# A prefix log-sum-exp kernel: the own-total addition moved from VectorE to TensorE, Ln put ahead of Exp, and the last step joined to the pipeline

## Chip, cores, metric

One core of one Trainium2 chip. The time is device microseconds of one execution; the reported figure is the median of several. Executions of one kernel agree within about 0.3%, so differences of 1 us need several rounds.

## The reference

```python
def reference(x):                      # x: (4, 4096, 4128) float32
    out[:, 0, :] = x[:, 0, :]
    for t in range(1, S):
        mx = np.maximum(out[:, t - 1, :], x[:, t, :])
        out[:, t, :] = mx + np.log(np.exp(out[:, t - 1, :] - mx) + np.exp(x[:, t, :] - mx))
```

It is a running log-sum-exp along the sequence. The kernel computes it as Exp, prefix sum, Ln. 270.5 MB go in and 270.5 MB come out.

## The kernel before

A step is 384 rows of one batch (four of the 44 steps have 256): partition p holds three consecutive rows, so a partition's own rows are summed on VectorE (DVE), and the sum over the partitions above comes from TensorE (PE) with a triangular matrix. Four column chunks of 1024 make a step; the last 32 columns ("tail") ride with one of them. Four step buffers; all transfers are issued from SyncE (SP).

```python
        def own(self):
            r = self.t.r
            full = tpool.tile([P, CH + tail], FP32R, name="tot")     # 2 buffers
            self.tot = full[:, :self.b - self.a]
            for j in range(1, r - 1):
                add(self.row(j), self.row(j - 1), self.row(j))
            add(self.tot, self.row(r - 2), self.row(r - 1))          # total of a partition
        # head():  PSUM above[c] (+)= excl.T @ tot   (and pick.T @ carry for the last chunk)

        def sums(self, a, b, p, cr):
            t = self.t
            n = t.r - 1
            if n:
                v = t.xt[:, :n, a:b]
                add(v, v, p.unsqueeze(1).to_broadcast(v.shape))      # all rows but the last
            add(t.xt[:, n, a:b], self.tot[:, a - self.a:b - self.a], p)   # last row: DVE
            if cr is not None and not t.final:
                nc.vector.tensor_copy(cr[96:, :], t.xt[96:, n, a:b])      # carry, from SBUF
        # complete():  PSUM above[c] += rest.T @ tot   (ready for the next step)
        ...
    for part in (steps[:-1], steps[-1:]):          # the last step is a drain of its own
        chunks = [Chunk(s, c) for s in part for c in order]
        N = len(chunks)
        for g in range(-2, N + 1):
            if 0 <= g + 2 < N:
                chunks[g + 2].act(ACT.Exp)         # may wait for a load
            if 0 <= g + 1 < N:
                chunks[g + 1].own()
                chunks[g + 1].head()
            if 0 <= g < N:
                chunks[g].add_above()
                ...
                chunks[g].complete()
            ...
            if 0 <= g - 1:
                result(chunks[g - 1])              # Ln; after a step's last chunk: store, next load
```

The softmax here doesn't subtract the row's maximum and nothing guards it: scores larger than these inputs give would overflow.

## Time and profile before

| | before |
|---|---|
| median of the first three runs | 1265.25 us (1265.19 to 1268.24) |
| span of the profiled run | 1262.5 us |
| busy DVE / ACT / PE | 81% / 73% / 38% |
| HBM traffic over the span | 429 GB/s |

A busy share is an average and says nothing of who waits for whom. Here I add only the landing of the last full step's load (the moment its data have arrived, and the first Exp on them starts) and the two last stores on SP's queue (columns: start us, duration us, queue and line, operation, tile):

```profile
1197.23 2.84 ACT L118 ACTIVATE xt<-xt 128x3168 f32<-128x3168 f32 x1 [7.74 <-DMA xt<-in_x_dram]
```

```profile
1231.79 0.33 SPq L106 DMA_DIRECT2D out_dram<-xt  x1
```

```profile
1250.60 0.33 SPq L106 DMA_DIRECT2D out_dram<-xt  x1
```

The span ends 11.9 us after the last of them.

### The profile page before, as it was taken

To read this page: it belongs to the slowest core of one execution; us is meant where nothing else is said; L and a number is where in the kernel's file an instruction comes from. 1 tells how busy PE (TensorE), PEld (TensorE's weight loads), DVE (VectorE), ACT (ScalarE), POOL (GpSimd) and SP (SyncE) were. 2 spreads that over 40 slices of the span, in tenths; PEclk is the share of its full clock that TensorE was granted. 3 is DMA by queue.
4 is the path that set the end of the run, shared out by engine and by line. 5 is a ranking of instruction groups with operands and counts; after the bars stand their busy time and mean duration, and the time that the engine had idled before them with its cause. 6 is when DMAs were issued, how large, how long until landed. Compare 5 with 4: busy or idle time off the path is not lost.

```text
span 1262.5 us, 3545 instructions
## 1 busy us (share of the span) xinstructions
PE 480.5 (38%) x876; PEld 220.3 (17%) x876; DVE 1024.4 (81%) x858; ACT 921.0 (73%) x353; POOL 1.5 (0%) x10
## 2 busy tenths in 40 slices
PE   2445433333334434443324434443432443444332
PEld 1212111111111112211111112111111211111111
DVE  4999878888888888888679888887867988887784
ACT  4986677777777776668669776666966977666784
POOL 0000000000000000000000000000000000000000
PEclk9865555565555555556556565656555656555656
DMA  9999999999999999999999999999999999999997
GB/s 410 410 444 431 426 433 438 432 430 435 436 427 430 443 432 429 435 437 432 433 435 429 429 441 432 428 437 435 424 425 431 434 433 432 430 436 433 433 409 340
DMA packets 12692, 541.29 MB, mean 429 GB/s; under 512 B 1408, under 2 KB 1408, under 8 KB 1408
## 3 DMA queue, kind: packets, MB, share of 16 engines
q1 hardware_dynamic: 12672, 541.07, 99.4%
q8 instruction: 7, 0.11, 0.0%
q14 instruction: 13, 0.11, 0.0%
HBM read 270.53 MB, written 270.53 MB: 429 GB/s over the span
## 4 chain that ended last, share of the span: by engine, by line
DMA 69%; ACT 19%; issue 7%; DVE 3%; SPq 0%; PE 0%; DVEq 0%; ACTq 0%
DMA xt<-in_x_dram 63%; ACT xt L118 19%; DMA out_dram<-xt 6%; DVE xt L86 3%; DVE tot L86 1%; SPq L106 0%; PE above L83 0%; DVE carry L155 0%; DVEq L239 0%; ACTq L118 0%; DVE carry_t L155 0%; DVEq L86 0%
## 5 line engine op out<-in xcount | busy, mean ns | idle before, releaser
L118 ACT ACTIVATE xt<-xt 128x3072 f32<-128x3072 f32 (+3 forms) x352 | 919.7, 2692 | 328.8 <-DMA xt<-in_x_dram 315.0
L83 PE MATMUL above<-tot,excl 128*128 128x512 f32 (+1 forms) x396 | 255.1, 714 | 476.9 <-DVE tot L86 472.6
L86 DVE TENSOR_TENSOR xt<-xt,above 128x2048 f32<-128x2048 f32 (+3 forms) x220 | 393.4, 1788 | 0.0
L86 DVE TENSOR_TENSOR xt<-xt 128x1024 f32<-128x1024 f32 (+1 forms) x160 | 197.0, 1231 | 179.9 <-ACT xt L118 177.5
L86 DVE TENSOR_TENSOR tot<-xt 128x1024 fp32r<-128x1024 f32 (+1 forms) x176 | 217.1, 1234 | 40.4 <-ACT xt L118 18.9
L86 DVE TENSOR_TENSOR xt<-tot,above 128x1024 f32<-128x1024 f32 (+1 forms) x220 | 221.5, 1007 | 0.0
L83 PEld LDWEIGHTS above<-tot,excl 128*128 128x128 f32 x396 | 104.4, 305 | 607.4 <-DVE tot L86 566.9
L83 PE MATMUL above<-tot,rest 128*128 128x512 f32 x240 | 129.2, 633 | 205.1 <-DVE xt L86 205.1
L83 PE MATMUL above<-carry,pick 128*128 128x512 f32 x160 | 139.5, 972 | 0.0
L83 PEld LDWEIGHTS above<-tot,rest 128*128 128x128 f32 x240 | 53.1, 276 | 295.9 <-DVE xt L86 294.1
L83 PE MATMUL above<-carry_t,pick 128*128 128x32 f32 x80 | 25.2, 409 | 83.2 <-DVE xt L86 83.2
L83 PEld LDWEIGHTS above<-carry,pick 128*128 128x128 f32 x160 | 51.5, 322 | 11.1
L83 PEld LDWEIGHTS above<-carry_t,pick 128*128 128x128 f32 x80 | 20.2, 311 | 110.3 <-DVE xt L86 108.3
L155 DVE COPY carry<-xt 32x1024 f32<-32x1024 f32 x40 | 27.6, 691 | 1.4
L155 DVE COPY carry_t<-xt 32x32 f32<-32x32 f32 x40 | 7.1, 178 | 1.4
L63 ACT ACT_TABLE_LOAD x1 | 1.3, 1283 | 0.8 <-PEq L228 0.8
L77 DVE MEMSET carry<- 128x1024 f32 x1 | 0.9, 912 | 1.1 <-PEq L228 1.1
L24 POOL TENSOR_SCALAR_AFFINE_SELECT rest<-rest 128x128 fp32r<-128x128 f32 x1 | 0.3, 293 | 0.0
L24 POOL TENSOR_SCALAR_AFFINE_SELECT pick<-pick 128x128 f32<-128x128 f32 x1 | 0.3, 292 | 0.1
L24 POOL TENSOR_SCALAR_AFFINE_SELECT excl<-excl 128x128 fp32r<-128x128 f32 x1 | 0.3, 292 | 0.0
L23 POOL MEMSET excl<- 128x128 f32 x1 | 0.2, 204 | 0.3 <-POOLq L228 0.3
L23 POOL MEMSET rest<- 128x128 f32 x1 | 0.2, 204 | 0.0
(6 smaller groups left out, 0.7 us busy)
## 6 DMA issues: line engine op xcount, KB each, us to landing
xt<-in_x_dram SPq DMA_DIRECT2D x40, 6192.0 KB, 41.9
out_dram<-xt SPq DMA_DIRECT2D x40, 6192.0 KB, 27.7
xt<-in_x_dram SPq DMA_DIRECT2D x4, 4128.0 KB, 37.0
out_dram<-xt SPq DMA_DIRECT2D x4, 4128.0 KB, 25.4
```

The source lines that it names most:

```text
L23: nc.gpsimd.memset(t.bitcast(FP32), 1.0 - fill)
L24: nc.gpsimd.affine_select(out=t, in_=t, pattern=[[step, P]], compare_op=op, fill=fill, base=base, channel_multiplier=-step if step else 1,)
L63: nc.scalar.preload_act_table_set("natural_log_exp_and_others")
L77: nc.vector.memset(carry, 0.0)
L83: nc.tensor.matmul(o, lhsT=w, rhs=rhs, start=start, stop=True, skip_group_check=True)
L86: nc.vector.tensor_tensor(out=o, in0=a, in1=b, op=mybir.AluOpType.add)
L118: nc.scalar.activation(v, v, func)
L155: nc.vector.tensor_copy(cr[96:, :], t.xt[96:, n, a:b])
```

## The change

The intent: DVE, the busiest compute engine, should no longer add a partition's own total to the sum above. PE adds it into PSUM with an identity matrix, and ScalarE (ACT) reads the last row of Ln straight from PSUM. The old `rest` matrix (totals at and below) becomes `below`, applied after Ln has read. Ln is put ahead of the Exp that may wait for a load, and the last step is no longer a drain of its own.

```diff
-        select(FP32R, 0.0, ge, 0, -1, "rest"),
+        select(FP32R, 0.0, ge, -1, -1, "below"),
+        select(FP32R, 1.0, ne, 0, 1, "ident"),
 ... (tail total in a small tile of its own, tail sums in a function of their own)
-            add(t.xt[:, n, a:b], self.tot[:, a - self.a:b - self.a], p)
-            if cr is not None and not t.final:
-                nc.vector.tensor_copy(cr[96:, :], t.xt[96:, n, a:b])
+        def add_own(self):
+            self.banks(ident)
+        def keep(self):
+            if self.c == lastc and not self.t.final:
+                nc.vector.tensor_copy(carry[96:, :], above[lastc][96:, :])
+        def ln(self):
+            t, n, a, b = self.t, self.t.r - 1, self.a, self.a + CH
+            v = t.xt[:, :n, a:b]
+            nc.scalar.activation(v, v, ACT.Ln)
+            nc.scalar.activation(t.xt[:, n, a:b], above[self.c], ACT.Ln)
 ...
-    for part in (steps[:-1], steps[-1:]):
-        ... Exp(g+2); own, head(g+1); add_above(g); complete(g); Ln(g-1)
+    chunks = [Chunk(s, c) for s in steps for c in order]
+    for g in range(-2, N + 1):
+        ... ln(g-1); complete(g-1); store; exp(g+2); own(g+1); keep(g-1);
+            add_above(g); add_own(g); total(g+1); head(g+1)
```

More of the change, by code (lines that the diff above doesn't have):

```diff
@@ L64 @@
     consts = ctx.enter_context(tc.tile_pool(name="consts", bufs=1))
-    excl, rest, pick = _constants(nc, consts)
+    excl, below, ident, pick = _constants(nc, consts)
     bufs = 4
@@ L69 @@
     tpool = ctx.enter_context(tc.tile_pool(name="tpool", bufs=2))
+    upool = ctx.enter_context(tc.tile_pool(name="upool", bufs=1))
     cpool = ctx.enter_context(tc.tile_pool(name="cpool", bufs=1))
@@ L114, in row, with exp @@
             return self.t.xt[:, j, self.a:self.b]
-        def act(self, func):
+        def exp(self):
             v = self.t.xt[:, :, self.a:self.b]
-            nc.scalar.activation(v, v, func)
+            nc.scalar.activation(v, v, ACT.Exp)
         def own(self):
-            r = self.t.r
-            full = tpool.tile([P, CH + tail], FP32R, name="tot")
-            self.tot = full[:, :self.b - self.a]
-            for j in range(1, r - 1):
+            for j in range(1, self.t.r - 1):
                 add(self.row(j), self.row(j - 1), self.row(j))
-            add(self.tot, self.row(r - 2), self.row(r - 1))
@@ L129, in banks, with total @@
-        def banks(self):
+        def total(self):
+            x, r, a = self.t.xt, self.t.r, self.a
+            self.tot = tpool.tile([P, CH], FP32R, name="tot")
+            add(self.tot, x[:, r - 2, a:a + CH], x[:, r - 1, a:a + CH])
+            if self.c == firstc:
+                self.t.tot_t = upool.tile([P, tail], FP32R, name="tot_t")
+                add(self.t.tot_t, x[:, r - 2, t0:], x[:, r - 1, t0:])
+        def banks(self, w, cr=None, start=False):
             for s in range(0, CH, MM):
-                yield above[self.c][:, s:s + MM], s, s + MM
+                o = above[self.c][:, s:s + MM]
+                if cr is not None:
+                    mm(o, pick, cr[:, s:s + MM], start=True)
+                mm(o, w, self.tot[:, s:s + MM], start=start)
@@ L133, in head @@
         def head(self):
             through = self.c == lastc and not self.t.first
-            for o, s, e in self.banks():
-                if through:
-                    mm(o, pick, carry[:, s:e], start=True)
-                mm(o, excl, self.tot[:, s:e], start=self.t.first)
-        def tail_head(self):
-            if not self.t.first:
-                mm(above_t, pick, carry_t, start=True)
-            mm(above_t, excl, self.tot[:, CH:], start=self.t.first)
-        def sums(self, a, b, p, cr):
-            t = self.t
-            n = t.r - 1
-            if n:
-                v = t.xt[:, :n, a:b]
-                add(v, v, p.unsqueeze(1).to_broadcast(v.shape))
-            add(t.xt[:, n, a:b], self.tot[:, a - self.a:b - self.a], p)
-            if cr is not None and not t.final:
-                nc.vector.tensor_copy(cr[96:, :], t.xt[96:, n, a:b])
@@ L157, in add_above @@
-        def add_above(self):
-            self.sums(self.a, self.a + CH, above[self.c], carry if self.c == lastc else None)
-            if self.c == firstc:
-                self.sums(t0, D, above_t, carry_t)
+            self.banks(excl, carry if through else None, start=self.t.first)
+        def add_above(self):
+            t, n = self.t, self.t.r - 1
+            v = t.xt[:, :n, self.a:self.a + CH]
+            add(v, v, above[self.c].unsqueeze(1).to_broadcast(v.shape))
+        def add_own(self):
+            self.banks(ident)
@@ L162, in complete @@
+        def keep(self):
[6 more added lines that the diff above has]
+            nc.scalar.activation(t.xt[:, n, a:b], above[self.c], ACT.Ln)
         def complete(self):
             if self.c != lastc and not self.t.final:
-                for o, s, e in self.banks():
-                    mm(o, rest, self.tot[:, s:e])
+                self.banks(below)
@@ L168, with tail_sums @@
+    def tail_sums(t):
+        n = t.r - 1
+        if not t.first:
+            mm(above_t, pick, carry_t, start=True)
+        mm(above_t, excl, t.tot_t, start=t.first)
+        v = t.xt[:, :n, t0:]
+        add(v, v, above_t.unsqueeze(1).to_broadcast(v.shape))
+        add(t.xt[:, n, t0:], t.tot_t, above_t)
+        if not t.final:
+            nc.vector.tensor_copy(carry_t[96:, :], t.xt[96:, n, t0:])
     steps = []
@@ L184 @@
     stored = 0
-    def result(k):
-        nonlocal stored
-        k.act(ACT.Ln)
-        if k.c == lastc:
-            k.t.store()
-            if bufs <= stored + ahead < len(steps):
-                steps[stored + ahead].load()
-            stored += 1
-    for part in (steps[:-1], steps[-1:]):
-        chunks = [Chunk(s, c) for s in part for c in order]
-        N = len(chunks)
-        for g in range(-2, N + 1):
-            if 0 <= g + 2 < N:
-                chunks[g + 2].act(ACT.Exp)
-            if 0 <= g + 1 < N:
-                chunks[g + 1].own()
-                chunks[g + 1].head()
-            if 0 <= g < N:
-                chunks[g].add_above()
-                if g + 1 < N and chunks[g + 1].c == firstc:
-                    chunks[g + 1].tail_head()
-                chunks[g].complete()
-            elif g == -1:
-                chunks[0].tail_head()
-            if 0 <= g - 1:
-                result(chunks[g - 1])
+    chunks = [Chunk(s, c) for s in steps for c in order]
+    N = len(chunks)
+    for g in range(-2, N + 1):
+        if 0 <= g - 1:
+            k = chunks[g - 1]
+            k.ln()
+            if k.c == order[1]:
+                v = k.t.xt[:, :, t0:]
+                nc.scalar.activation(v, v, ACT.Ln)
+            k.complete()
+            if k.c == lastc:
+                k.t.store()
+                if bufs <= stored + ahead < len(steps):
+                    steps[stored + ahead].load()
+                stored += 1
+        if g + 2 < N:
+            chunks[g + 2].exp()
+        if 0 <= g + 1 < N:
+            chunks[g + 1].own()
+        if 0 <= g - 1:
+            chunks[g - 1].keep()
+        if 0 <= g < N:
+            chunks[g].add_above()
+            chunks[g].add_own()
+            if chunks[g].c == order[1]:
+                tail_sums(chunks[g].t)
+        if 0 <= g + 1 < N:
+            chunks[g + 1].total()
+            chunks[g + 1].head()
 _INS = ['x']
```

## The prediction

> **What bounds the kernel now.** I read the page's DMA rows first, then the busy table, who waited for whom, and last the stretches of time at both ends.
>
> ```profile
> span 1262.5 us, 3545 instructions
> PE 480.5 (38%) x876; PEld 220.3 (17%) x876; DVE 1024.4 (81%) x858; ACT 921.0 (73%) x353; POOL 1.5 (0%) x10
> ...
> DMA  9999999999999999999999999999999999999997
> ...
> HBM read 270.53 MB, written 270.53 MB: 429 GB/s over the span
> ...
> L86 DVE TENSOR_TENSOR xt<-tot,above 128x1024 f32<-128x1024 f32 (+1 forms) x220 | 221.5, 1007 | 0.0
> ```
>
> DVE at 81% looks like the engine to relieve, and the last line is the work that the change takes from it. But the DMA row is at nine tenths in every slice but the last. The stretches say how near to its limit that is (columns: stretch, length, busy PE, PEld, DVE, ACT, POOL with counts, then PE clock, DMA share, GB/s):
>
> ```profile
> 97.00:1197.00 1100.00, 425.71 (x772) 194.43 (x772) 904.04 (x751) 803.29 (x304) 0.00 (x0) 0.56 1.00 433
> ...
> 1229.00:1231.00 2.00, 0.00 (x0) 0.00 (x0) 0.00 (x0) 2.00 (x1) 0.00 (x0) 0.50 0.34 149
> ...
> 1232.00:1246.00 14.00, 7.41 (x15) 3.71 (x15) 11.60 (x12) 10.89 (x6) 0.00 (x0) 0.58 1.04 449
> ...
> 1247.00:1250.00 3.00, 0.00 (x0) 0.00 (x0) 1.57 (x2) 2.65 (x2) 0.00 (x0) 1.00 0.04 17
> ```
>
> For 1100 us the queue runs at 433 GB/s and never pauses. It does pause at the end, twice: about 1228.7 to 1232.3 and 1246.6 to 1251.0 (read from half-microsecond stretches), because there the next store has not been issued. Who waits confirms it:
>
> ```profile
> ACT xt L118 <- DMA xt<-in_x_dram: 315.0, 41, 12.4
> ...
> DVE xt L86 <- ACT xt L118: 177.5, 35, 12.2
> ```
>
> ACT idles some 7.7 us in each step for a load, DVE behind it. A full step moves 2 x 6.34 MB (6192 KB in, the same out); at 433 GB/s this is 29.3 us, and loads do land 29.25 us apart (ACT starts on them at 1108.58 and 1137.83).
>
> How much queue is left when ACT is late? The load landing at 1197.2 (call it L) and the store queue near it:
>
> ```profile
> 1184.13 0.33 SPq L106 DMA_DIRECT2D out_dram<-xt  x1
> 1184.52 0.42 SPq L103 DMA_DIRECT2D xt<-in_x_dram  x1
> ```
>
> A load lands 42 us after its issue (page, transfers), of which only 14.6 are its own at 433 GB/s: the rest is queue. With the store issued 13 us before a landing and the following load right behind it, about 29 us of work is queued when a load lands; the next store comes 16.2 us later (1213.37 - 1197.2). So some 13 us of queue remain at the leanest moment of a step. Compute is not on the path in the middle; it is only at the end, where no load is left.
>
> **What the Trainium skill says.** "DMA: Bandwidth & Descriptors", section "Where 436 GB/s comes from", gives 435 GB/s as the ceiling of the 16 SBUF ports. The 433 GB/s measured here agrees: nothing on compute engines can raise it. "ScalarE: Activation LUTs", section "What ACT_TABLE_LOAD costs", gives 186 ns + 0.833 ns per element for an activation with immediates, and 93 ns overlap of neighbours. This trace: 1896 ns at 2048, 2748 at 3072 (formula 1892 and 2745), and eight in a row take 21.50 us where their own durations sum to 22.17, so 96 ns of overlap. Thus 1024 elements should take 1.04 us, 96 should take 0.27; whether a PSUM source costs the same no run shows. "TensorE: Matmul & The Clock Gate", section "What's actually happening", says that the array clock halves unless PE has lately been busy; here the mean granted clock is 0.584 and a pair of 512-column matmuls takes 1.22 us at half clock, 0.73 right after the carry matmuls.
>
> **The change part by part.**
> (1) Removed from DVE: 176 adds tot + above of 1214 ns = 213.6 us. Added: 44 small tail totals of 0.18 = 8 us; the 44 totals of 1258 shrink to 1225 (-1.5). DVE falls from 1024 to about 819 us, 24 to 19 us per step. All of it lies beside DMA: worth 0 in the middle.
> (2) PE gains 352 identity matmuls with 352 weight loads. At 633 to 756 ns (the rest and excl groups) that is +220 to +265 us, PE near 720 us, 57%. It is below the transfers' time, but in the chain: the second Ln of a chunk waits for it.
> (3) ACT: each Ln of 3072 (2.75) becomes 2048 from SBUF (1.90) and 1024 from PSUM (1.04); the tail becomes a separate 0.27. Per full step 13 activations: 2.84 + 3 x 2.75 + 4 x 2.94 + 0.27 = 23.1, less 12 overlaps of 0.095 = 22.0 us against 21.5 now; ACT some 950 us in all. Hidden under 29.3.
> (4) The sum below now waits for Ln of the same chunk (it overwrites what Ln reads), and the next total but one needs the buffer that it frees. A new ring: total 1.2, excl 1.2, add 2.3, identity 1.2, Ln 1.0 to 2.9, below 1.2. It spans two chunks, about 10 us, so 5 per chunk.
> (5) Ln goes ahead of Exp. A store now comes after the load's landing + Exp 2.84, Ln 2.9, Exp 2.7, Ln 2.9 = 11.3 us instead of 16.2. In the middle this only lengthens the queue from 13 to 18 us. The load behind it then waits for the previous store's landing, about L + 14.8, which is still in time.
> (6) The last step is no longer a drain of its own.
>
> Middle: I walked one step through the orders of the engines by hand with the durations above, from a landing at 0. Ln of the four chunks start at 14.0, 19.6, 26.3, 33.3 (the second and third held up by the tail's matmuls and adds and by the carry matmuls), the first again one step later at about +26. So 26 of 29.3 us: DMA-bound as before, with less room than the busy times suggest.
>
> Start: the first store waits now for Exp of the second load before its last Ln: 41.3. By the same walk it comes at about 37.8, and the dip to 264 GB/s at 56 to 58 may fill: -0.7 us at most.
>
> End, where time can change, counted from L = 1197.2. The queue then holds work until L + 31.5 (drained at 1228.7), in both kernels. The last load lands at L + 24.3 (37.0 us after 1184.5). Walk of the changed kernel: last full step's second chunk, Ln to 22.8; Exp of the last step 24.3 to 26.3; Ln of the third chunk to 29.2; carry and excl matmuls of the fourth to 31; add to 33.2; Ln 33.3 to 36.2. Store at L + 36.2; before, 1231.8 = L + 34.6. It fills the queue from 36.7 to 51.1 (14.4 as before). Then the last step, three and more rounds of total 1.2 + excl 1.2 + add 1.2 with handoffs, the tail's 1.7, the carry matmuls 3.3, ending with Ln in two parts at L + 55.6; before, 1250.6 = L + 53.4. Its store moves data from 56.0 to 65.6 (9.6 as before), and the end is 1.9 later: 67.5 against 65.3 now.
>
> Sum: 0 (middle) - 0.7 (start) + 2.2 (end) = +1.5 us: 1265.25 + 1.5 = 1266.75; I say 1266.5.
>
> **Rivals.**
> (a) The end becomes better: Exp of the last step can start at its load's landing, not 10 us later. If nothing else held, both gaps (3.6 and 4.4 us) would close: 1257. For it: order of Exp. Against: the chain runs over DVE and PE, in order, not over Exp. A faster PE clock under more matmuls would take about 1 us off.
> (b) The new ring with its PE handoffs exceeds 29.3 us a step (it has 26 by hand; each of four chunks would need 0.8 us more, for instance by an Ln from PSUM far above 1.04). Then the bound moves from DMA to the ring, and 1 us of excess costs 40 us: 1300. Against: all but the PSUM Ln are measured durations, and DVE and ACT each have over 7 us of idle.
> (c) Freed DVE time shows in full (1024 - 819, so 5 us a step): 1060. This needs more than 435 GB/s; excluded by the DMA row.
>
> **Range and chances.** Spread of before is 3 us; my walk may be off by 3 us either way at the end. Range 1260 to 1272. A 2% gain is 1240, below the 1250 that 541 MB at 433 GB/s take alone (541.07 / 0.433 = 1249.6): 1%. Slower by 2% needs (b): 2%. Within: 97%.
>
> **What would show it.** DMA share 1.00 and 433 GB/s from 97 to 1197 again; DVE near 819, PE near 720, ACT near 950; more ACT idle waiting for loads per step or about the same (some 7 us); stores 11 to 12 us after the landing; first store near 38; at the end two DMA pauses of about 5 us, not 3.6 and 4.4. I am wrong if the loads' spacing departs from 29.25 us, if ACT waits for PE in the middle rather than for loads, or if the two pauses close.

## The result, and the profile after

| | before | after |
|---|---|---|
| median | 1265.22 us (4 runs) | 1266.87 us (4 runs, 1266.13 to 1267.86) |
| ratio, 95% interval | 1 | 1.0009 (0.9991 to 1.0028): the same |
| span of the profiled run | 1262.5 | 1264.4 |
| DVE / ACT / PE busy us | 1024.4 / 921.0 / 480.5 | 853.3 / 940.5 / 653.6 |

Ratios here and below are the mean of one kernel's fast runs over the mean of the other's fast runs of the same rounds, so they are not quite the ratio of the medians quoted. The experiments ran in three groups, two on one chip and the third (carry copy, total twice, pieces without the additions on PE) on another; each group has its own runs of the kernel before.

The page of the changed kernel: busy engines, the DMA row, and the groups that carry the change.

```profile
PE 653.6 (52%) x1228; PEld 331.8 (26%) x1228; DVE 853.3 (67%) x726; ACT 940.5 (74%) x573; POOL 1.9 (0%) x12
...
DMA  9999999999999999999999999999999999999997
...
L85 PE MATMUL above<-tot,ident 128*128 128x512 f32 x352 | 204.8, 681 | 336.3 <-DVE xt L88 336.0
L163 ACT ACTIVATE xt<-xt 128x2048 f32<-128x2048 f32 (+1 forms) x176 | 321.0, 1824 | 69.6 <-DVE xt L88 69.3
...
L164 ACT ACTIVATE xt<-above 128x1024 f32<-128x1024 f32 x176 | 177.5, 1008 | 0.9 <-PE above L85 0.9
...
L158 DVE COPY carry<-above 32x1024 f32<-32x1024 f32 x40 | 49.2, 1230 | 53.8 <-ACT xt L164 53.8
```

DVE lost 171 us of work and the DMA row did not change by a digit. The stretches of the changed kernel (columns as in the prediction), to be held against those of before:

```profile
97.00:1195.00 1098.00, 576.06 (x1080) 292.69 (x1079) 756.29 (x639) 823.59 (x498) 0.00 (x0) 0.56 1.00 433
...
1229.00:1232.00 3.00, 1.32 (x4) 0.44 (x4) 1.28 (x3) 3.00 (x3) 0.00 (x0) 0.99 0.15 66
1232.00:1247.00 15.00, 8.58 (x17) 4.89 (x18) 8.33 (x9) 9.48 (x9) 0.00 (x0) 0.50 0.98 423
1247.00:1253.00 6.00, 2.87 (x6) 0.79 (x4) 1.22 (x1) 1.97 (x2) 0.00 (x0) 0.78 0.04 17
```

The same 433 GB/s and share 1.00 for 1098 us, then two pauses again (66 and 17 GB/s). The landing and the two last stores of the changed kernel:

```profile
1195.72 2.85 ACT L120 ACTIVATE xt<-xt 128x3168 f32<-128x3168 f32 x1 [6.89 <-DMA xt<-in_x_dram]
```

```profile
1231.74 0.33 SPq L108 DMA_DIRECT2D out_dram<-xt  x1
```

```profile
1252.48 0.33 SPq L108 DMA_DIRECT2D out_dram<-xt  x1
```

The last but one is issued at the same time as before (1231.79), the last one 1.9 us later than 1250.60. The spans differ by 1.9 us. That is where the whole difference of the two traces lies. (The load of the last full step happened to land 1.5 us earlier, at 1195.72 instead of 1197.23, so counted from the landing both stores are later: 36.0 and 56.8 us against 34.6 and 53.4.)

What sets the time between that landing and the last store is in the chain of work that ended last (window 1198 to 1252 us; "issue" is time without a wait that the profile shows), first before, then changed:

```profile
by line: DVE xt L86 47.9%; ACT xt L118 15.8%; DVE tot L86 13.8%; issue 13.8%; DVE carry L155 2.6%; PE above L83 2.3%; DVEq L239 2.1%; DVE carry_t L155 0.3%; DVEq L86 0.2%; ACTq L118 0.1%
by line: PE above L85 40.0%; DVE xt L88 27.3%; ACT xt L163 12.5%; DVE tot L88 6.7%; issue 6.7%; ACT xt L164 5.1%; DVE carry L158 4.6%; ACTq L254 1.7%; DVE carry_t L180 0.3%; ACTq L163 0.1%
```

Before, it is mostly DVE, and PE has 2% of it; in the changed kernel PE has 40%.

### The profile page after: what moved, and what is told of

The parts are those of the page before. It is cut to its first block, busy times and chain, and to the rows that moved or that the text cites. A ratio compares the mean times of both kernels' runs of the same rounds, so it can differ in the third digit from the quotient of the medians.

```text
span 1264.4 us, 4467 instructions
## 1 busy us (share of the span) xinstructions
PE 653.6 (52%) x1228; PEld 331.8 (26%) x1228; DVE 853.3 (67%) x726; ACT 940.5 (74%) x573; POOL 1.9 (0%) x12
## 4 chain that ended last, share of the span: by engine, by line
DMA 75%; ACT 8%; DVE 6%; PE 6%; issue 4%; ACTq 0%; SPq 0%
DMA xt<-in_x_dram 47%; DMA out_dram<-xt 28%; PE above L85 6%; ACT xt L163 5%; DVE xt L88 4%; ACT xt L164 2%; DVE tot L88 2%; DVE carry L158 1%; ACT xt L120 0%; ACTq L254 0%; DVE carry_t L180 0%; SPq L108 0%; SPq L105 0%; ACTq L120 0%; ACTq L163 0%
## 5 line engine op out<-in xcount | busy, mean ns | idle before, releaser
L120 ACT ACTIVATE xt<-xt 128x3072 f32<-128x3072 f32 (+3 forms) x176 | 474.7, 2698 | 240.8 <-DMA xt<-in_x_dram 240.8
L88 DVE TENSOR_TENSOR xt<-xt,above 128x2048 f32<-128x2048 f32 (+2 forms) x220 | 394.8, 1795 | 136.5 <-PE above L85 135.2
L85 PE MATMUL above<-tot,ident 128*128 128x512 f32 x352 | 204.8, 681 | 336.3 <-DVE xt L88 336.0
L163 ACT ACTIVATE xt<-xt 128x2048 f32<-128x2048 f32 (+1 forms) x176 | 321.0, 1824 | 69.6 <-DVE xt L88 69.3
L85 PE MATMUL above<-tot,excl 128*128 128x512 f32 x352 | 263.7, 827 | 113.8 <-DVE tot L88 97.0
L88 DVE TENSOR_TENSOR tot<-xt 128x1024 fp32r<-128x1024 f32 x176 | 214.8, 1221 | 27.3 <-ACT xt L120 13.0
L85 PE MATMUL above<-tot,below 128*128 128x512 f32 x240 | 131.9, 648 | 147.5 <-ACT xt L164 147.4
L85 PEld LDWEIGHTS above<-tot,ident 128*128 128x128 f32 x352 | 87.2, 301 | 447.2 <-DVE xt L88 444.9
L164 ACT ACTIVATE xt<-above 128x1024 f32<-128x1024 f32 x176 | 177.5, 1008 | 0.9 <-PE above L85 0.9
L85 PEld LDWEIGHTS above<-tot,below 128*128 128x128 f32 x240 | 64.1, 303 | 215.6 <-ACT xt L164 204.1
L158 DVE COPY carry<-above 32x1024 f32<-32x1024 f32 x40 | 49.2, 1230 | 53.8 <-ACT xt L164 53.8
```

What stands on the lines that cost most here:

```text
L85: nc.tensor.matmul(o, lhsT=w, rhs=rhs, start=start, stop=True, skip_group_check=True)
L88: nc.vector.tensor_tensor(out=o, in0=a, in1=b, op=mybir.AluOpType.add)
L120: nc.scalar.activation(v, v, ACT.Exp)
L158: nc.vector.tensor_copy(carry[96:, :], above[lastc][96:, :])
L163: nc.scalar.activation(v, v, ACT.Ln)
L164: nc.scalar.activation(t.xt[:, n, a:b], above[self.c], ACT.Ln)
```

## Experiments

Theory: the transfers set the pace until the last load has landed; the compute of the changed kernel is paced by a ring of dependent work over DVE, PE and ACT (each waits for the one before it, and the first again for the last), not by the busy time of any engine, and this ring shows only at the end. Rivals are in the expectations. Twelve kernels were run.

### Both kernels with the transfers taken off the path

```diff
-            nc.sync.dma_start(out=self.dram(out), in_=self.xt)
+            nc.sync.dma_start(out=self.dram(out)[:, :, :512], in_=self.xt[:, :, :512])
```

This leaves most of the output unwritten, so the result is wrong.

> The kernel before with stores cut to the first 512 of 4128 columns (wrong output on purpose), so a full step moves 6.34 + 0.79 MB, 16.5 us at 433 GB/s, and the transfers cannot set the pace. My theory (transfers bind the real kernel, DVE is next): DVE 24 to 25 us a full step, 42.7 full steps' worth, plus about 30 us of ends: 1075 us, DVE over 95% busy. Rival (compute runs no faster than 29 us a step): 1250 or more.

> The changed kernel with the same cut. My theory: the ring total, excl, add, identity, Ln, below with its handoffs takes 26 us a step, so 42.7 x 26 + 30 = 1140 us, slower than the kernel before under the same cut, with no engine over 90%. Rival A (the ring already takes 29.3 us and only happens to match the transfers): 1250 or more. Rival B (the relief of DVE carries through, ACT with 22 us a step binds): about 980 us, faster than the cut kernel before by 100 us.

Measured: 1074.05 us for the kernel before, 1114.79 us for the changed one (one look each). The middle 800 us, first before, then changed:

```profile
200.00:1000.00 800.00, 357.10 (x664) 163.31 (x662) 780.79 (x651) 711.53 (x267) 0.00 (x0) 0.58 0.72 291
```

```profile
200.00:1000.00 800.00, 449.35 (x897) 232.49 (x897) 623.54 (x530) 692.57 (x418) 0.00 (x0) 0.59 0.68 279
```

With the cut stores the kernel before is bound by DVE: 780.79 of 800 us, 98%. In the changed kernel no engine is above 87% (ACT, 692.57 of 800), and yet it is slower by 41 us. What it waits for, in its view of waits (engine, line, tile, what it waited for; us in total, times, longest):

```profile
PE above L85 <- DVE xt L88: 354.0, 173, 4.8
DVE xt L88 <- PE above L85: 213.4, 173, 4.3
ACT xt L163 <- DVE xt L88: 153.0, 123, 3.4
```

DVE waits for PE and PE waits for DVE, both a couple of hundred microseconds, and ACT for DVE. The chain of work from 400 to 700 us shows the ring itself, first before, then changed:

```profile
by line: DVE xt L86 70.0%; DVE tot L86 16.9%; issue 5.4%; PE above L83 5.2%; DVE carry L155 2.5%; DVE carry_t L155 0.7%; DVEq L86 0.2%
by line: PE above L85 39.0%; DVE xt L88 36.6%; ACT xt L163 7.6%; DVE tot L88 5.3%; DVE carry L158 4.5%; ACT xt L164 3.7%; issue 2.3%; DVE carry_t L180 0.6%; ACT xt L120 0.6%; ACTq L163 0.1%; DVE tot_t L88 0.0%
```

Before, the chain is DVE for 90%. In the changed kernel it goes to and fro between DVE (47%), PE (39%) and ACT (12%): each waits its turn and none is full. The stores in this run are alternately 25.05 and 26.15 us apart over most of this stretch, so a step takes 25.6 us where the kernel before takes 24.65. Rival A (29.3) and rival B (22, ACT bound) both fall. So the change does not speed up the compute; it slows it by 1 us a step, and the real kernel does not show it in the middle because a step's transfers take 29.3 us.

### One part of the change undone: the last step a drain of its own again

```diff
+    for part in (steps[:-1], steps[-1:]):
-    chunks = [Chunk(s, c) for s in steps for c in order]
+        chunks = [Chunk(s, c) for s in part for c in order]
```

> The changed kernel with the last step again a drain of its own, as before (one part undone). My theory: middle unchanged (433 GB/s); the last but one store still comes 36 us after the landing of the last full step's load, but the last step's Exp only starts then, so the last store comes some 2 to 3 us later: +2.5 us over the changed kernel, 1269. Rival (joining the last step cost the time, because its Exp stands in the way): 1262 to 1264.

Measured: 1270.45 us, ratio to before 1.0048 (1.0035 to 1.006). The last but one store came 36.3 us after the landing, as expected, the last one 60.2 us (changed kernel 56.8). Joining the last step is worth 3.4 us to the changed kernel at the end (2 to 3 expected); the rival falls.

### One part undone: Exp ahead of Ln again

```diff
     for g in range(-2, N + 1):
+        if g + 2 < N:
+            chunks[g + 2].exp()
         if 0 <= g - 1:
             ... ln, complete, store
-        if g + 2 < N:
-            chunks[g + 2].exp()
```

> The changed kernel with Exp again ahead of Ln (one part undone). My theory: in the middle stores come about 17 us after a landing instead of 11, the queue still never empties, so no change there; at the end the last but one store comes some 5 us later (41 instead of 36 us after the landing), and so does the last: +5 us, 1272. Rival 1 (order of Ln and Exp matters nowhere because the chain runs over DVE and PE alone): 1267. Rival 2 (the ring becomes too slow for the transfers in the middle): 1300 or more.

Measured: 1276.43 us, ratio 1.0097 (1.0081 to 1.0112): the direction is right, the size too small. The end is as walked: 42.2 us after the landing for the last but one store (41 expected), 63.0 for the last. What I had left out is the start, where compute is still behind the loads. These are the stretches there:

```profile
66.00:67.00 1.00, 0.19 (x1) 0.00 (x0) 0.65 (x1) 1.00 (x2) 0.00 (x0) 1.00 0.23 99
...
66.00:80.00 14.00, 6.33 (x14) 3.67 (x14) 11.38 (x11) 12.98 (x10) 0.00 (x0) 0.56 0.93 400
80.00:97.00 17.00, 9.18 (x17) 4.32 (x16) 12.94 (x11) 12.90 (x7) 0.00 (x0) 0.60 1.09 423
97.00:110.00 13.00, 8.36 (x18) 4.88 (x19) 10.81 (x12) 12.19 (x8) 0.00 (x0) 0.50 0.85 368
110.00:1195.00 1085.00, 531.87 (x1058) 271.83 (x1057) 741.62 (x626) 812.18 (x489) 0.00 (x0) 0.58 1.00 433
```

The second store is issued at 67.21 us instead of 63.14, and just before it the queue runs dry: 99 GB/s from 66 to 67 us, where the changed kernel has 347. The third is issued at 93.47 instead of 88.25, and from 97 to 110 us 368 GB/s are moved instead of 427; there the packets' own durations leave no engine idle, so this second loss is not explained. The later landings are 3 to 4 us later (the one of the last full step 1198.88 instead of 1195.72). From 110 us on it is 433 GB/s as everywhere. So with the additions on PE, Ln first pays: some 3 us at the start and 6 at the end, in one trace of each.

### The other parts alone, on the kernel before

Only the last step joined (`for part in (steps,)`):

> The kernel before with only the last step joined to the others (no drain of its own). My theory, by the same walk: Exp of the last step stands ahead of the last Ln of the step before, so the last but one store comes at about 38 us after the landing of the last full step's load instead of 34.6; the last store's data are then ready (49 us) before that store has left the queue (53), so the second pause goes. -0.5 us, 1264 (the same within noise). Rival (joining is what cost the changed kernel its time): 1267 to 1269.

Measured: 1263.8 us, ratio 0.9988 (0.9974 to 1.0002). The last two stores came 38.0 and 49.8 us after the landing (38 and 49 expected): the first pause is longer and the second is nearly gone. The rival falls.

Only Ln ahead of Exp (`result(chunks[g - 1])` moved to the top of the loop body):

> The kernel before with only Ln put ahead of Exp, drain kept. My theory: first store at about 37 instead of 41 us, worth under 1 us; in the middle only a longer queue; end as before (its last two stores 34.6 and 53.4 us after that landing): 1264, the same. Rival (Ln first frees buffers earlier and speeds up the middle): below 1255.

Measured: 1264.88 us, ratio 0.9996 (0.9983 to 1.0008). The first store came at 38.20 instead of 41.31, the middle stayed at 433 GB/s, the last two stores came 34.6 and 54.4 us after the landing. The rival falls.

Both together, that is the changed kernel without the additions on PE and what comes with them (Ln in two parts, the tail apart, `below` after Ln, a chunk's total behind the addition above it):

> The kernel before with Ln ahead of Exp and the last step joined, that is the changed kernel without the additions on TensorE (two of three parts). My theory: last but one store at 35 us after that landing, last store's data at 49 us, before the queue is through with the one before: second pause gone, -3.5 us against before, 1261; so the additions on TensorE alone cost the changed kernel some 5 us at the end. Rival (the additions on TensorE cost nothing, and the order and the join made the +2 us): 1266 to 1267.

Measured: 1263.47 us, ratio 0.9983 (0.9971 to 0.9996). Right in direction; smaller than expected, because the last two stores came 36.7 and 50.8 us after the landing where I had 35 and 49:

```profile
1234.18 0.33 SPq L106 DMA_DIRECT2D out_dram<-xt  x1
```

```profile
1248.27 0.33 SPq L106 DMA_DIRECT2D out_dram<-xt  x1
```

The end is 64.2 us after the landing (1197.5), in the changed kernel 68.7: the additions on PE, with what comes with them, cost 4.5 us there. Which of these parts weighs how much was not separated, but for the carry copy below. In the times it is 0.9983 against 1.0009, some 3 us, from different groups of runs and with intervals that just overlap; the two spans differ by 2.7 us, because the changed kernel's load landed 1.8 us earlier.

### The carry copy

The copy of the carry row is the one DVE operation that got slower, and in the page it waits 53.8 us for ACT. Ln of the same chunk reads the same PSUM tile, and the copy starts only when that Ln has ended. DVE around one step's carry copy in the changed kernel:

```profile
1203.96 1.23 DVE L88 TENSOR_TENSOR xt<-xt 128x1024 f32<-128x1024 f32 x1
1206.67 1.23 DVE L158 COPY carry<-above 32x1024 f32<-32x1024 f32 x1 [1.49 <-ACT xt L164]
1207.93 2.29 DVE L88 TENSOR_TENSOR xt<-xt,above 128x2048 f32<-128x2048 f32 x1
```

DVE idles 1.49 us for a copy whose source PE had finished earlier (the identity matmuls ended at about 1203.4; Ln ended at 1206.64), and the next addition queues behind it. Moved to right after the next chunk's total, ahead of Ln:

```diff
-        if 0 <= g - 1:
-            chunks[g - 1].keep()
 ...
             chunks[g + 1].total()
             chunks[g + 1].head()
+        if 0 <= g < N:
+            chunks[g].keep()
```

> The changed kernel with the carry copy moved from after Ln of its chunk to right after the next chunk's total, and with stores cut to 512 columns as in a_narrow (wrong output on purpose). In a_narrow the copy waited 28 us in all for Ln, since both read the same PSUM and the program orders them. My theory (the ring of DVE and PE sets the pace there, and this wait is in it): 1114.8 - 28 = 1087 us, with some back for the Ln that now waits for the copy: 1085 to 1100. Rival (ACT sets the pace): 1113 or more.

> The same move with full stores. My theory: no change in the middle; at the end the copy no longer delays the last step's first addition (it ended 37.3 us after the landing of the last full step's load), so the last store comes 1 to 1.5 us earlier: 1265.5. Rival (the wait for the copy is hidden at the end too): 1267.

Measured with cut stores: 1099.59 us, at the edge of the expectation: 15 us less than 1114.79 (one look each, on two chips). The wait turned round: Ln now waits for the copy, 37 times and 19.2 us in all, so the program keeps the two reads apart whichever comes first. These 19.2 us against the 28 saved explain the direction of the shortfall and not its size, as other waits changed too (Ln's for DVE's additions fell from 153.0 to 117.5 us). Measured with full stores: 1265.08 us, ratio to before 0.9998 (0.9986 to 1.0011). The last store came 54.9 us after the landing instead of 56.8, the last but one 36.4 instead of 36.0. The end gained 1.9 us where 1 to 1.5 was expected; in these traces moving the copy takes back more than half of the 3.4 us by which the changed kernel's last store trails that of before. The times agree in direction (0.9998, against 1.0009 for the changed kernel), but their intervals overlap widely.

### How near the ring is to the transfers

```diff
             add(self.tot, x[:, r - 2, a:a + CH], x[:, r - 1, a:a + CH])
+            add(self.tot, x[:, r - 2, a:a + CH], x[:, r - 1, a:a + CH])
```

> The changed kernel with every total computed twice (same values, one more DVE add of 1.22 us a chunk, 4.7 us a step). DVE had over 9 us of idle in each step. My theory (the ring takes 25.6 us of 29.3 and the add lies in it): 30.3 us a step less what is absorbed where ACT sets the pace of a chunk, so the middle becomes just slower than the transfers, DMA share under 1: 1280 to 1320. Rival (idle DVE time is free): 1267 plus about 5 at the end, 1272, DMA share still 1.00.

Measured: 1277.59 us, ratio 1.0095 (1.0078 to 1.0112), between the two expectations, and my theory's number is missed. The middle, and ACT's wait for loads over the whole run (changed kernel: 240.8 us in 41 waits):

```profile
97.00:1195.00 1098.00, 535.89 (x1079) 287.64 (x1079) 943.25 (x797) 841.83 (x503) 0.00 (x0) 0.58 1.00 432
```

```profile
ACT xt L120 <- DMA xt<-in_x_dram: 62.5, 24, 11.0
```

The transfers still just set the pace: ACT has almost no wait for loads left. So 4.7 us more in a step brought the ring up to about the transfers' 29.3, not beyond; some of it must have been absorbed, as 25.6 + 4.7 is 30.3. The cost came at the ends: the landing of the last full step's load at 1199.90 (4 us late, most of it lost before 97 us, where the rate was 406 GB/s against 421 in the changed kernel; the second store is issued at 68.58 instead of 63.14), and the last store 61.8 us after it (56.8 in the changed kernel). The rival "idle DVE time is free" is right for the middle and for the 5 us that it gave the end; it had no loss at the start. Two of the four runs (1279.48 and 1279.99) are 4 us longer than the traced one (1275.35); why, no trace shows.

### Stores of the last two steps in pieces

```diff
+            late = k.t in steps[-2:]
+            if late: k.t.store(k.a, k.b)      # this chunk's columns only
             if k.c == lastc:
+                if not late:
                     k.t.store()
```

(In the changed kernel the first chunk's piece waits for the tail's Ln and is issued with the second.)

> The changed kernel with the stores of the last two steps issued chunk by chunk, as Ln finishes each. My theory: the pauses at the end fill with the pieces and behind the last Ln (56 us after that landing) only a quarter of 9.6 us is left: end 61 to 62 instead of 68.7 us after the landing, -7 us against the changed kernel, 1260. Rival (small stores with 4 KB runs move slower, or the end is set by something other than the late stores): 1266 or more.

> The best so far (b_merged_ln) with the stores of the last two steps in pieces as in a_pieces. There the pauses filled but the pieces moved at about 400 GB/s and the last of them ended 8.2 us before nothing else was left, instead of 11.9. My theory: last Ln about 51 us after the landing, end 59 to 60: 1258 to 1260, 0.5% under before. Rival (the pieces' lower rate takes back what the filled pauses give): 1263.

Measured: 1264.5 us, ratio 0.9992 (0.998 to 1.0005), for the changed kernel with pieces; 1263.68 us, ratio 0.9982 (0.9969 to 0.9996), for the best one so far with pieces, which is no better than without (0.9983). The expectations of 1260 and of 1258 to 1260 were both missed. The trace of the latter shows why:

```profile
1229.00:1253.00 24.00, 7.90 (x13) 3.55 (x13) 15.48 (x16) 14.88 (x8) 0.00 (x0) 0.50 1.00 407
1254.00:1262.80 8.80, 0.00 (x0) 0.00 (x0) 0.00 (x0) 0.00 (x0) 0.00 (x0) 0.50 0.12 50
```

The pauses are gone (share 1.00, at 407 GB/s and not 433), and nearly all data are out at 1254. But then 50 GB/s trickle for 8.8 us at a DMA share of 0.12, that is about two of 16 engines' worth: the engines do not finish evenly. The rival's outcome came, in part for its reason (24 us at 407 instead of 433 GB/s are some 1.4 us, an estimate) and mostly for this one.

The pieces are not what makes engines lag. The same kernel without pieces has the same trickle in its first pause, before the last but one store is issued at 1234.18:

```profile
1230.00:1232.00 2.00, 0.82 (x3) 0.72 (x3) 1.94 (x3) 0.61 (x1) 0.00 (x0) 0.50 0.12 50
```

Counted with their durations, the packets there keep one to three of the 16 engines at work until 1235. With whole stores a pause follows in which these engines catch up; with pieces none follows, and the lag stands at the end. This reading fits both traces but was not tested, and why some engines lag stays open.

### The ends side by side

Times counted from the landing of the last full step's load, read from the traces:

| kernel | landing | last but one store | last store | end | ratio to before |
|---|---|---|---|---|---|
| before | 1197.2 | 34.6 | 53.4 | 65.3 | 1 |
| before, joined | 1198.0 | 38.0 | 49.8 | 64.5 | 0.9988 |
| before, Ln first | 1197.5 | 34.6 | 54.4 | 66.3 | 0.9996 |
| before, both | 1197.5 | 36.7 | 50.8 | 64.2 | 0.9983 |
| changed | 1195.7 | 36.0 | 56.8 | 68.7 | 1.0009 |
| changed, carry copy moved | 1196.2 | 36.4 | 54.9 | 66.8 | 0.9998 |
| changed, drain kept | 1196.6 | 36.3 | 60.2 | 72.1 | 1.0048 |
| changed, Exp first | 1198.9 | 42.2 | 63.0 | 74.9 | 1.0097 |
| changed, total twice | 1199.9 | 39.7 | 61.8 | 73.7 | 1.0095 |

Where the last store is ready before the queue is through with the one before it (the second and fourth row), the end is set by the queue and lies 13 to 15 us after that store; in all others it follows by 11.9.

## Why the prediction was right

The predicted time was 1266.5 us, the measured median 1266.87; the change is the same as before within noise, as was forecast at 97%. Step by step:

**The middle, 0 us: right.** 433 GB/s and share 1.00 in both traces, loads 29.3 us apart (ACT starts on them at 1107.25 and 1136.54). The runs with cut stores show directly that compute has room: 25.6 us a step with the cut, where the walk by hand had 26. Stores came 10.9 us after a landing (1206.66 against 1195.72), predicted 11.3.

**The start, -0.7 us: not shown, and the dip was misread.** The first store came at 36.91 (predicted 37.8), but from 56 to 58 us the changed kernel moves the same 264 GB/s, as does every run with full stores. That dip is no pause: a stretch counts a packet whole where it starts (so short stretches can show a share above 1), and the next one, 58 to 66 us, has 450 GB/s at a share of 1.04 in both kernels. Counted with their durations, the packets of both kernels keep the 16 engines busy there, so nothing was left to fill. Over the first 97 us both move 421 GB/s. The landing of the last full step's load was 1.5 us earlier than before in these two traces. Other traces of the changed kernel with Ln first have it at 1196.2, 1196.6 and 1197.4; the kernel before with Ln first, whose first store is early too (38.20), had it at 1197.5, no earlier than before. How much of the 1.5 us is scatter stays open.

**The end, +2.2 us: right in sign and mechanism, too small.** Counted from the landing, the last but one store was predicted at 36.2 and came at 36.0; the last was predicted at 55.6 and came at 56.8; the end was predicted at 67.5 and came at 68.7, so +3.4 against before. The term that was missed is the carry copy: the walk does not list it. It takes 1.23 us instead of 0.69, now that its source is PSUM, and it waits for Ln; moving it took back 1.9 us, more than the 1.2 us by which the walk was short, so some other term must have been off the other way. "VectorE: DVE Perf Modes", section "Why PSUM operands drop a tier", has it that an fp32 operand in PSUM holds a copy to the slowest mode, and the runs agree: the carry copy of 32x1024 takes 691 ns from SBUF and 1230 ns from PSUM. I had not looked it up. The two pauses were predicted at about 5 us each; they were about 3 and 6, 8.7 in sum against 8.0 before (both read from stretches that count a packet where it starts, so some engines are still at work in them).

**The sum: close in part by luck.** The prediction had -0.7 + 2.2 = +1.5 us; the two traces have -1.5 + 3.4 = +1.9. The error at the end and the earlier landing cancel in part. The interval of the times, 0.9991 to 1.0028, runs from 1.1 us faster to 3.5 us slower, so the times alone do not show even the sign.

**Busy times: ACT right, DVE and PE off.** ACT 940.5 for "some 950". DVE 853.3 for 819 (the prediction's own terms give 817): the 40 carry copies are 1230 ns instead of 691 (+21.6 us), and the rest is overlap: before, the durations of DVE's instructions sum to 1064.7 us in 1024.4 busy, after to 879.6 in 853.3, so the removed additions took 14 us of overlap with them. PE 653.6 for 720: the identity matmuls are 681 ns each, inside the 633 to 756 assumed, but overlap their neighbours to 204.8 us in all. None of it reached the time.

**ACT waiting for loads: some 7 us a step predicted, 240.8 / 41 = 5.9 measured (315.0 / 41 = 7.7 before).** The rest went into waits of Ln for DVE (69.3 us in all), the ring at work in the middle, under the transfers.

**The rivals.** (a) Closing pauses: not in the changed kernel; in the kernel before with the last step joined and Ln first, the second one closes nearly, for 0.17% in all. (b) The ring above 29.3 us: no, but 4.7 us more in a step bring it there. (c) The freed DVE time in full: no.

## What to carry to other kernels

Where the transfers run without a pause, as here at 433 GB/s for 1098 us, relieving the busiest engine can move only the ends, and the chain of work there decides the sign. Moving work to an idle engine can lengthen the chain of handoffs even where it leaves no engine full: with the stores cut, DVE fell from 98% to 78% and the time rose by 41 us. A cheap check before such a change is to cut the transfers and see whether the compute really gets faster.

## What the Trainium skill lacked or had wrong

- "ScalarE: Activation LUTs", section "What ACT_TABLE_LOAD costs", gives 186 ns + 0.833 ns per element for an activation with immediates and does not say in which memory the source lies. For 1024 elements it gives 1039 ns; the runs show 1040 to 1060 ns for such an Ln from SBUF and 1008 ns (mean of 176) from PSUM.
- "DMA: Bandwidth & Descriptors", section "Measured (HBM→SBUF, 128 partitions, SWDGE, issued from GpSimd)", advises batches of at least 1 MiB and has numbers for loads alone. Stores of 1024 to 1584 KB in 4 KB runs, several in a row, moved at 397 to 407 GB/s here against 433 for the whole-step mix. At their end 50 GB/s trickled for 8.8 us at a DMA share of 0.12, and whole stores left the same trickle ahead of a pause. No page has a figure for how far apart the 16 engines end.
